# Moving the four adds of one pooling group from GpSimd to VectorE in a hybrid decoder step

## The chip, the cores and the metric

The kernel runs on one core of a Trainium2 chip. The metric is the device time of one execution in microseconds (us), taken as the median of several runs; lower is better. The core has five engines with queues of their own: TensorE (PE in the profile, its weight loads PEld), VectorE (DVE), ScalarE (ACT), GpSimd (POOL) and SyncE (SP), which here only issues DMAs.

## The reference

One inference step of a decoder trunk with one layer: a half-step SwiGLU FFN, a mixer, a second half-step FFN and a final RMSNorm, for one sequence of 512 new tokens and for 8 samples with one token each (520 tokens in all, 1024 features, float32). The mixer has two parallel parts, a Mamba-2 state-space part (SSD) and the pooling part that the change touches:

```python
POOL_WINDOWS = (2, 4, 8, 16)
...
    u = jnp.concatenate([prefix.astype(u_new.dtype), u_new], axis=1)
    cs = jnp.cumsum(u.astype(jnp.float32), axis=1)
    cs = jnp.concatenate([jnp.zeros((b, 1, POOL_DIM), jnp.float32), cs], axis=1)
    end = cs[:, POOL_STATE + 1:]
...
    for gi, w in enumerate(POOL_WINDOWS):
        sl = slice(gi * POOL_GROUP_DIM, (gi + 1) * POOL_GROUP_DIM)
        start = POOL_STATE + 1 - w
        win_sum = end[..., sl] - cs[:, start:start + T, sl]
        cnt = jnp.minimum(w, pos + 1).astype(jnp.float32)
        outs.append(win_sum / cnt[None, :, None])
    pooled = jnp.concatenate(outs, axis=-1) - u_new.astype(jnp.float32)
```

Each of four groups of 128 channels takes the mean over its last 2, 4, 8 or 16 tokens, minus the token itself. The result goes through a 128x128 matrix for each group, and then with the SSD part through the output projection `w_out`.

## The kernel before

Features lie on the 128 partitions and tokens along the free dimension, in two halves of 260 tokens (`HALVES`). Every float32 product of a weight and an activation is made of three matmuls on split operands (`mm3`, lines 123 to 128): a weight tile `raw` is rounded to `whi` by ScalarE (L113), and the rest `wlo = raw - whi` is made by VectorE (L114). The kernel runs FFN 1, the mixer and FFN 2 one after the other; TensorE is the engine that hardly pauses.

The mixer is a list of steps written out by hand. The strings `CONV_PLAN`, `GATE_PLAN` and `LAST_PLAN` name them in order, and `run` calls them:

- `p0` to `p3`: `pooling(g)`, a projection `inproj` of one group (48 matmuls into two PSUM banks), its copy to the tile `PU` by VectorE (`evac`, L703 to L705), and the window sums. For a window of 16, four adds with steps 1, 2, 4 and 8 make tiles `PW3_1`, `PW3_2`, `PW3_4` and `PW3_8`, each 128 partitions by about 650 elements. Then GpSimd mends the first tokens (L827, L828) and copies the new state out (L829, L830).
- `c0` to `c3`: `centre`, mean minus token (VectorE L834, L838, ScalarE L837). `m0` to `m3`: `mix`, the 128x128 product (L844 to L847).
- `A0` to `A7`: `ssd_a` for one chunk of 128 tokens and one of two head groups: two banks `pb` and `px` are filled by TensorE, a tile `ab` of 128x1024 is loaded by DMA (L954) and turned into decays by VectorE (L971), ScalarE (L969, L973, L974) and a last product on VectorE (L980); VectorE makes `xdt` from `px` (L976) and GpSimd makes `we` (L958) and `xw` (L979).
- `B0` to `B7`: `ssd_b`: TensorE makes `yo`, `pst` and `yd` from these; GpSimd scales the state `hst` (L1001), VectorE adds to it (L1002), puts `yo` and `yd` together in `E` (L1005, L1006) and adds into `X` (L1009).
- `z0` to `z7`: gate projections (tiles `inz`), 48 matmuls each, evacuated by VectorE (L1019). `o`, `g` and `h`: the output projection `w_out` in three blocks of four steps (`wout`, tiles `wo`), each half of a feature block added to `h` by VectorE (L1029). The block `g` (`wo1`) is followed by `h` (`wo2`) in `LAST_PLAN`.

The change sits in `p3`. The steps around it, as the plans give them:

```python
    "c3 X1 m2 A3 B2 e0"
...
    "A4 z0 B3 z1 m3 z2 B4 z3 s2 A5 ...
```

Two things decide the order on the engines. First, the whole program is recorded and then put in order at build time by a scheduler with a timeline model of its own (`schedule_with_timeline_sim=True`); each engine then runs its list strictly in order. An edit of one instruction's engine can so reorder other instructions. Second, all PSUM tiles of the mixer come from one pool of eight banks (`ppm`, through `bank`). The first matmul into a tile waits until the last reader of the bank's former tile is done. Which former tile that is comes from the same build-time model.

Of the kernel before, what the change touches and what calls it, by code (L numbers as in the profile page):

```python
# [12 lines left out]
ALU = mybir.AluOpType  # L13
# [37 lines left out]
LP = SAMPLE_P + 16 * NS  # L51
# [610 lines left out]
def mixer(tc, ins, outs, e):  # L662
    nc = tc.nc
# [29 lines left out]
    def inproj(src, name):  # L693
        wh, wl = load_unit(src, D, f"in{name}")
        bs = [bank(f"in{name}{b}") for b in range(2)]
        for b, hs in enumerate(HALVES):
            for k in range(KD):
                mm3(bs[b][:, :HB], ws(wh, k), ws(wl, k), xh[:, k, hs], xl[:, k, hs], k == 0, k == KD - 1)
        return bs

    def evac(bs, buf, off, soff, sstep):
        nb = SEQ - HB
        nc.vector.tensor_tensor(out=buf[:, off : off + HB], in0=bs[0][:, :HB], in1=r[:, :HB], op=ALU.mult)  # L703
        nc.vector.tensor_tensor(out=buf[:, off + HB : off + SEQ], in0=bs[1][:, :nb], in1=r[:, HB:SEQ], op=ALU.mult)
        nc.vector.tensor_tensor(out=buf[:, soff : soff + sstep * (NS - 1) + 1 : sstep], in0=bs[1][:, nb:HB],  # L705
                                in1=r[:, SEQ:NT], op=ALU.mult)
# [104 lines left out]
    def pooling(g):  # L811
        w = WINDOWS[g]
        bs = inproj(ins["w_in"][12 + g], f"p{g}")
        U = cv[0].tile([P, LP], F32, tag="cu", bufs=6, name=f"PU{g}")
        us = U[:, SAMPLE_P:LP].rearrange("p (b j) -> p b j", j=16)
        nc.gpsimd.memset(U[:, 0:PAST], 0.0)
        nc.gpsimd.tensor_copy(us[:, :, 0:PAST], spool[:, g])
        evac(bs, U, PAST, SAMPLE_P + PAST, 16)
        cur, step = U, 1
        while step < w:  # L820
            nxt = cv[0].tile([P, LP], F32, tag="cu", bufs=6, name=f"PW{g}_{step}")
            lo = 2 * step - 1
            nc.gpsimd.tensor_tensor(out=nxt[:, lo:LP], in0=cur[:, lo:LP], in1=cur[:, lo - step : LP - step], op=ALU.add)
            cur, step = nxt, 2 * step
        first = slice(PAST, PAST + w - 1)
        sx = slice(SAMPLE_P + PAST, LP, 16)
        nc.gpsimd.tensor_tensor(out=cur[:, first], in0=cur[:, first], in1=rcnt[:, : w - 1], op=ALU.mult)  # L827
        nc.gpsimd.tensor_tensor(out=cur[:, first], in0=cur[:, first], in1=U[:, first], op=ALU.subtract)  # L828
        nc.gpsimd.tensor_copy(npp[:, g], U[:, SEQ : SEQ + PAST])  # L829
        nc.gpsimd.tensor_copy(spool[:, g], us[:, :, 1:16])  # L830

        def centre():
            for q in (slice(PAST + w - 1, PAST + SEQ), sx):
                nc.vector.scalar_tensor_tensor(out=cur[:, q], in0=cur[:, q], scalar=1.0 / w, in1=U[:, q],  # L834
                                               op0=ALU.mult, op1=ALU.subtract)
            for q, t in ((slice(PAST, PAST + SEQ), slice(0, SEQ)), (sx, slice(SEQ, NT))):
                nc.scalar.copy(catp[:, 0, g, t], cur[:, q])  # L837
                nc.vector.tensor_tensor(out=catp[:, 1, g, t], in0=cur[:, q], in1=catp[:, 0, g, t].bitcast(F32),  # L838
                                        op=ALU.subtract)

        def mix():
            for b, hs in enumerate(HALVES):
                ps = bank(f"pm{g}{b}")
                mm3(ps[:, :HB], ws(wph, g), ws(wpo, g), catp[:, 0, g, hs], catp[:, 1, g, hs], True, True)  # L844
                sc = v("pool_scale", g)
                nc.scalar.activation(out=catp[:, 0, g, hs], in_=ps[:, :HB], func=AF.Copy, scale=sc)
                nc.vector.scalar_tensor_tensor(out=catp[:, 1, g, hs], in0=ps[:, :HB], scalar=sc,  # L847
                                               in1=catp[:, 0, g, hs].bitcast(F32), op0=ALU.mult, op1=ALU.subtract)
        return centre, mix
# [225 lines left out]
    def outs_a():  # L1075
# [10 lines left out]
        "y": lambda j: sample_bc(),  # L1086
        "X": sample_x,
        "p": lambda j: pooled.append(pooling(j)),
        "c": lambda j: pooled[j][0](),
        "m": lambda j: pooled[j][1](),  # L1090
# [112 lines left out]
```

## Time and profile before

| | before |
|---|---|
| median of 3 runs | 988.39 us (987.58 to 988.75) |
| profiled execution, time | 988.96 us |
| its span in the profile | 987.1 us |
| TensorE matmul, busy | 971.9 us (98%) |
| VectorE, busy | 797.2 us (81%) |
| ScalarE, busy | 555.2 us (56%) |
| GpSimd, busy | 91.2 us (9%) |

The span is the stretch from the first to the last instruction of the profiled execution; 1.86 us of its 988.96 us lie outside of it. A timeline row gives the start of an instruction, or of several alike that follow each other (xN), the time that it took, engine, line, operation, output<-input, and in brackets how long the engine had been idle and what ended that. Instructions of one engine overlap by some 0.07 us at their ends, so the distance from one start to the next is a little less than the duration.

### The profile page before, as it was taken

To read this page: it belongs to the slowest core of one execution; us is meant where nothing else is said; L and a number is where in the kernel's file an instruction comes from. 1 tells how busy PE (TensorE), PEld (TensorE's weight loads), DVE (VectorE), ACT (ScalarE), POOL (GpSimd) and SP (SyncE) were. 2 spreads that over 40 slices of the span, in tenths; PEclk is the share of its full clock that TensorE was granted. 3 is DMA by queue.
4 is the path that set the end of the run, shared out by engine and by line. 5 is a ranking of instruction groups with operands and counts; after the bars stand their busy time and mean duration, and the time that the engine had idled before them with its cause. 6 is when DMAs were issued, how large, how long until landed. Compare 5 with 4: busy or idle time off the path is not lost.

```text
span 987.1 us, 19460 instructions
## 1 busy us (share of the span) xinstructions
PE 971.9 (98%) x7868; PEld 952.7 (97%) x7868; DVE 797.2 (81%) x1287; ACT 555.2 (56%) x1019; POOL 91.2 (9%) x161
## 2 busy tenths in 40 slices
PE   9999999999999999999999999999999999999996
PEld 8999999999999999999899999999999999999995
DVE  6999656996569688789978997999967899668876
ACT  7766414664236465685668574666643566534653
POOL 0000000000000000156522000100012000120000
PEclk9999999999999999999999999999999999999998
DMA  7523232323222232262335232523346423453212
GB/s 217 178 86 124 90 100 72 129 86 129 86 86 97 75 126 99 86 192 100 122 114 187 77 131 86 154 101 128 121 118 195 146 99 116 123 179 124 92 64 88
DMA packets 43963, 116.57 MB, mean 118 GB/s; under 512 B 6552, under 2 KB 14680, under 8 KB 43872
## 3 DMA queue, kind: packets, MB, share of 16 engines
q1 hardware_dynamic: 39824, 104.18, 31.3%
q0 software_dynamic: 3776, 11.01, 4.3%
q8 instruction: 62, 1.02, 0.4%
q14 instruction: 29, 0.24, 0.1%
q10 hardware_dynamic: 272, 0.13, 0.0%
HBM read 107.96 MB, written 7.34 MB: 117 GB/s over the span
## 4 chain that ended last, share of the span: by engine, by line
PE 89%; DVE 4%; ACT 3%; DMA 1%; issue 1%; POOL 0%; SPq 0%; DVEq 0%; ACTq 0%
PE A L128 8%; PE A L124 8%; PE A L127 8%; PE dn L128 7%; PE dn L124 7%; PE dn L127 7%; PE BE L128 6%; PE BE L127 6%; PE BE L124 6%; PE wo L124 2%; PE wo L128 2%; PE wo L127 2%; PE P L257 2%; PE inz L124 2%; PE inz L128 2%; PE inz L127 2%
## 5 line engine op out<-in xcount | busy, mean ns | idle before, releaser
L124 PE MATMUL dn<-g,whi_1d 128*128 128x260 f32 x352 | 99.5, 283 | 0.2 <-DVE td L421 0.2
L127 PE MATMUL dn<-g,whi_1d 128*128 128x260 f32 x352 | 99.7, 283 | 0.0
L128 PE MATMUL dn<-g,wlo_1d 128*128 128x260 f32 x352 | 99.4, 282 | 0.0
L421 DVE SCALAR_TENSOR_TENSOR td<-dn,r_f 128x520 f32<-128x520 f32 x40 | 27.9, 699 | 72.8 <-PE dn L128 72.8
L128 PE MATMUL dn<-g,wlo_2d 128*128 128x260 f32 x256 | 72.7, 284 | 1.0 <-DVE wlo_2d L114 1.0
L127 PE MATMUL dn<-g,whi_2d 128*128 128x260 f32 x256 | 72.4, 283 | 0.0
L124 PE MATMUL dn<-g,whi_2d 128*128 128x260 f32 x256 | 72.4, 283 | 0.0
L124 PEld LDWEIGHTS dn<-g,whi_1d 128*128 128x128 f32 x352 | 66.2, 188 | 0.4 <-DVE td L421 0.4
L128 PEld LDWEIGHTS dn<-g,wlo_1d 128*128 128x128 f32 x352 | 66.4, 189 | 0.0
L127 PEld LDWEIGHTS dn<-g,whi_1d 128*128 128x128 f32 x352 | 66.3, 188 | 0.0
L351 ACT COPY ac<-A 128x260 f32<-128x260 f32 x123 | 45.5, 372 | 28.7 <-PE A L128 27.2
L113 ACT CAST whi_1d<-raw_1d 128x1024 fp32r<-128x1024 f32 (+1 forms) x24 | 23.4, 980 | 67.1 <-PE dn L127 54.3
L312 DVE TENSOR_TENSOR s<-raw 128x1024 f32<-128x1024 f32 x39 | 47.6, 1221 | 5.8 <-DMA raw<-in_w2gu 5.8
L128 PEld LDWEIGHTS dn<-g,wlo_2d 128*128 128x128 f32 x256 | 48.2, 188 | 1.2 <-DVE wlo_2d L114 1.2
L124 PEld LDWEIGHTS dn<-g,whi_2d 128*128 128x128 f32 x256 | 48.4, 189 | 0.0
L127 PEld LDWEIGHTS dn<-g,whi_2d 128*128 128x128 f32 x256 | 48.3, 189 | 0.0
L257 PE MATMUL P<-xg_f,raw 128*128 128x260 f32 x192 | 44.2, 384 | 0.8 <-ACT tg L270 0.6
L257 PEld LDWEIGHTS P<-xg_f,raw 128*128 128x128 f32 x192 | 35.8, 190 | 6.7 <-ACT tg L270 1.0
L124 PE MATMUL wo<-catg,whi_wo 128*128 128x260 f32 x128 | 37.2, 291 | 0.0
L124 PE MATMUL inz<-xh_mx,whi_inz 128*128 128x260 f32 x128 | 36.8, 288 | 0.1
L124 PE MATMUL inx<-xh_mx,whi_inx 128*128 128x260 f32 x128 | 36.5, 285 | 0.0
L128 PE MATMUL wo<-catg,wlo_wo 128*128 128x260 f32 x128 | 36.2, 283 | 0.0
(1351 smaller groups left out, 3954.8 us busy)
## 6 DMA issues: line engine op xcount, KB each, us to landing
raw<-in_w2gu SPq DMA_DIRECT2D x44, 512.0 KB, 4.5
raw<-in_w1gu SPq DMA_DIRECT2D x41, 512.0 KB, 4.4
raw_1d<-in_w1d SPq DMA_DIRECT2D x16, 512.0 KB, 4.4
raw_2d<-in_w2d SPq DMA_DIRECT2D x16, 512.0 KB, 4.4
raw_wo<-in_w_out SPq DMA_DIRECT2D x12, 512.0 KB, 4.6
ab<-scr_acs SPq DMA_DIRECT2D x8, 512.0 KB, 4.3
h<-in_state_ssm SPq DMA_DIRECT2D x16, 256.0 KB, 3.4
raw_inz<-in_w_in SPq DMA_DIRECT2D x8, 512.0 KB, 4.0
```

The lines of the kernel that those rows point to most:

```text
L113: cast = nc.scalar.copy(h, src)
L124: first = nc.tensor.matmul(ps, whi, xhi, start=start, stop=False, **kw)
L127: nc.tensor.matmul(ps, whi, xlo, start=False, stop=False, **kw)
L128: nc.tensor.matmul(ps, wlo, xhi, start=False, stop=stop, **kw)
L257: mm = nc.tensor.matmul(self.banks[f, u][b][:, :HB], ws(self.raw[f][:, u], j + 4 * q), xg[:, slot[q]], start=j == q == 0, stop=j == 3 and ...
L312: nc.vector.tensor_tensor(out=s1, in0=diag, in1=up0, op=ALU.add)
L351: nc.scalar.copy(keep, out[:, :HB])
L421: nc.vector.scalar_tensor_tensor(out=t, in0=banks[d][:, :, :HB], scalar=-0.5, in1=self.nx[3].rearrange("p (b t) -> p b t", b=2), op0=ALU.mult,
```

## The change

In `pooling`, the adds of group 3 (window 16) are issued to VectorE; those of groups 0 to 2 stay on GpSimd. Nothing else is edited. From line 824 on, the changed kernel's line numbers are higher by one.

```diff
         while step < w:
             nxt = cv[0].tile([P, LP], F32, tag="cu", bufs=6, name=f"PW{g}_{step}")
             lo = 2 * step - 1
-            nc.gpsimd.tensor_tensor(out=nxt[:, lo:LP], in0=cur[:, lo:LP], in1=cur[:, lo - step : LP - step], op=ALU.add)
+            eng = nc.vector if g == 3 else nc.gpsimd
+            eng.tensor_tensor(out=nxt[:, lo:LP], in0=cur[:, lo:LP], in1=cur[:, lo - step : LP - step], op=ALU.add)
             cur, step = nxt, 2 * step
```

## Prediction
> **What bounds the kernel now.** I read the page first: the busy times, then the chain that ended last.
>
> ```profile
> PE 971.9 (98%) x7868; PEld 952.7 (97%) x7868; DVE 797.2 (81%) x1287; ACT 555.2 (56%) x1019; POOL 91.2 (9%) x161
> ...
> PE 89%; DVE 4%; ACT 3%; DMA 1%; issue 1%; POOL 0%; SPq 0%; DVEq 0%; ACTq 0%
> ```
>
> TensorE is busy nearly all the time and makes 89% of the chain. VectorE's 81% and GpSimd's 9% matter only where TensorE waits for them. So I asked for TensorE's waits between 440 and 600 us, the mixer, and then for its timeline where they are.
>
> ```profile
> 476.98 1.09 PE L995 MATMUL yd<-ab,xdt 128*64 128x128 f32 x16 [0.43 <-DVE U L703]
> ...
> 478.65 0.30 PE L944 MATMUL pb<-ident,BC 128*128 128x128 f32 x1 [0.58 <-DVE U L705]
> ...
> 479.83 0.55 PE L952 MATMUL px<-ident,X 128*128 128x128 f32 x3 [0.66 <-DVE xdt L976]
> 480.43 0.39 PE L124 MATMUL inz<-xh_mx,whi_inz 128*128 128x260 f32 x1
> ```
>
> In brackets stand the only three: 0.43, 0.58 and 0.66 us, 1.67 us in all, each ended by VectorE. All are bank waits. The `yd` of step B2 and the `pb` of A4 take the banks whose last readers are the copies L703 and L705 of the projection `inx`; the `px` of A4 takes the bank that `xdt` L976 reads. The `inz` at 480.43 (z0) starts without a gap, but in the built program its bank is the one that `yo` of B2 held, read by L1005. So VectorE's queue is late here and TensorE is held by it. Its timeline at that place, with the clean durations of the same operations from later on:
>
> ```profile
> 465.00 0.17 DVE L705 TENSOR_TENSOR PU<-inp,r_mx 128x8 f32<-128x8 f32 x1
> ...
> 465.67 2.00 DVE L114 TENSOR_TENSOR wlo_inz<-raw_inz,whi_inz 128x1024 fp32r<-128x1024 f32 x1
> ...
> 468.50 1.40 DVE L980 TENSOR_TENSOR ab<-ab,scm 128x1024 f32<-128x1024 f32 x1
> ...
> 470.84 0.69 DVE L1002 TENSOR_TENSOR hst<-pst,hst 128x512 f32<-128x512 f32 x1 [0.34 <-POOL hst L1001]
> 471.45 2.61 DVE L1009 SCALAR_TENSOR_TENSOR X<-X,h,E 128x128 f32<-128x128 f32 x4
> 474.76 1.83 DVE L971 TENSOR_SCALAR ab<-ab,tok 128x128 f32<-128x128 f32 x2 [0.70 <-ACT E L964]
> 476.51 0.42 DVE L703 TENSOR_TENSOR U<-inx,r_mx 128x260 f32<-128x260 f32 x1
> 476.85 1.25 DVE L971 TENSOR_SCALAR ab<-ab,tok 128x128 f32<-128x128 f32 x6
> ...
> 479.70 0.68 DVE L1005 TENSOR_TENSOR E<-yo,E 128x512 f32<-128x512 f32 x1
> 480.30 1.26 DVE L114 TENSOR_TENSOR wlo_inz<-raw_inz,whi_inz 128x1024 fp32r<-128x1024 f32 x1
> ...
> 484.36 1.12 DVE L1009 SCALAR_TENSOR_TENSOR X<-X,h,E 128x128 f32<-128x128 f32 x4
> 485.42 1.21 DVE L980 TENSOR_TENSOR ab<-ab,scm 128x1024 f32<-128x1024 f32 x1
> ...
> 500.30 0.86 DVE L971 TENSOR_SCALAR ab<-ab,tok 128x128 f32<-128x128 f32 x4
> ```
>
> L1005 (479.70) ends at 480.38, and `inz` starts 0.05 us later. L703 ends at 476.93, and `yd` starts 0.05 us later. So 0.05 us lies between a reader's end and the matmul.
>
> Many of these rows are too long. A 128x1024 product takes 1.21 (485.42), but 2.00 at 465.67. Four L1009 take 1.12 (484.36), but 2.61 at 471.45. Four L971 take 0.86 (500.30), but two take 1.83 at 474.76. GpSimd's timeline says why:
>
> ```profile
> 465.31 1.27 POOL L823 TENSOR_TENSOR PW<-PU 128x654 f32<-128x654 f32 x1
> 466.53 1.28 POOL L830 COPY spool<-PU 128x120 f32<-128x120 f32 x1
> 467.78 1.04 POOL L979 TENSOR_TENSOR xw<-xdt,we 128x512 f32<-128x512 f32 x1
> 468.78 2.03 POOL L1001 TENSOR_TENSOR hst<-hst,cd 128x512 f32<-128x512 f32 x1
> 470.77 2.62 POOL L823 TENSOR_TENSOR PW<-PW 128x652 f32<-128x652 f32 x2
> 474.61 0.20 POOL L958 TENSOR_TENSOR we<-ab,tok 128x8 f32<-128x8 f32 x1 [1.23 <-DMA ab<-scr_acs]
> 474.77 1.54 POOL L823 TENSOR_TENSOR PW<-PW 128x640 f32<-128x640 f32 x1
> ...
> 479.44 1.04 POOL L1001 TENSOR_TENSOR hst<-hst,cd 128x512 f32<-128x512 f32 x1
> 480.44 2.02 POOL L979 TENSOR_TENSOR xw<-xdt,we 128x512 f32<-128x512 f32 x1
> ```
>
> The adds of the group stand at 465.31, 470.77 (two) and 474.77. The long VectorE rows start while an add runs and come free when it ends, and the reverse: `hst` (468.78, 2.03 against 1.04 at 479.44) waits for VectorE's product to end. [...] Rows with an operand in PSUM (L1005, 0.68) are not stretched.
>
> **The change, part by part.** *The order.* In the built programs TensorE has the same list in both. On VectorE the four adds go into the stretch between the last copy of `PU` (ends 465.17) and L703 (476.51). Besides, the scheduler reorders what follows: the split L114 of `inz` (480.30) now stands ahead of `xdt`, and so ahead of L1005; the four L971 of `ab` for A3 stand between `xdt` and L1005. ScalarE makes the decays of A4 first and those of A3 later. On SP one small output DMA goes ahead of one weight load. I take the end of L1005 as the clock of this place, because z0 cannot start before it, and count what VectorE has to do up to there.
>
> *Added: four adds.*
>
> ```profile
> L834 DVE SCALAR_TENSOR_TENSOR PW<-PW,PU 128x505 f32<-128x505 f32 x1 | 0.7, 689 | 0.4 <-POOL PW L823 0.4
> ...
> L312 DVE TENSOR_TENSOR s<-raw 128x1024 f32<-128x1024 f32 x39 | 47.6, 1221 | 5.8 <-DMA raw<-in_w2gu 5.8
> ```
>
> From 689 ns for 505 elements and 1221 for 1024 follow 1.03 ns an element, so 0.84 us for 654, and 0.76 from start to start: +3.0 us.
>
> *Moved ahead of L1005: the split L114.* 480.30 to 481.48, where the next instruction starts in the trace: +1.2 us.
>
> *Removed: the stretching by the adds.* L114 at 465.67, 2.00 - 1.26 = 0.74; the four L1009, 2.61 - 1.12 = 1.49; two L971, 1.75 from start to start against 0.4 = 1.35. Together -3.6 us.
>
> *Removed: two idle times of VectorE*, 0.34 for GpSimd's `hst` and 0.70 for ScalarE's `E`. GpSimd reaches `hst` earlier without the adds, and L971 no longer follows `E` at once: -1.0 us. Also the 0.19 us by which `xw` (467.78) stretched L980 at 468.50.
>
> *Added: new collisions.* GpSimd still has two `hst` and two `xw` of 1.04 us each, now against a VectorE with more SBUF work. The first pair starts about 466.1, when its small copies are over, and meets L114 and the second add. The second `hst` comes behind a copy that waits for L705 and so starts together with L834 and L114. The second `xw` waits for `xdt` alone and starts the moment it ends, where the four L971 stand. None of this is in the trace of before; the bounds are nothing and all four whole, 4.2 us. The rows say that who comes first holds the other for what is left, so more than half: I take 0.9 for the first pair, 0.6 and 0.9 for the others, 2.4 us.
>
> The sum: 480.38 + 3.0 + 1.2 - 3.6 - 1.0 - 0.2 + 2.4 = 482.2, and z0 starts at about 482.2 instead of 480.43: **+1.8 us**, in which the three waits are contained. TensorE does not win the 1.67 us: the first two waits shrink or go, and one before `inz` takes their place. With the bounds: 479.8 and 484.0, so -0.6 to +3.5 us.
>
> *Does ScalarE hold VectorE there?*
>
> ```profile
> 474.09 1.28 ACT L964 ACTIVATE E<-ab 64x512 f32<-64x512 f32 x2 [3.04 <-DVE X L1009]
> ...
> 476.68 1.26 ACT L969 ACTIVATE ab<-ab,tok 128x128 f32<-128x128 f32 x4
> 477.85 1.03 ACT L113 CAST whi_inz<-raw_inz 128x1024 fp32r<-128x1024 f32 x1
> ```
>
> The `ab` of A4 has landed when GpSimd's `we` starts at 474.61. In the new order ScalarE then makes `we`, four L969 (1.26) and the `whi` cast (1.03): about 477.2, when VectorE, at my count, reaches the split. It is just in time and costs nothing; if the load of `ab` lands late (on SP it stands behind a weight load that waits for the L114 of 465.67), each us of it counts here, since `xdt` stands behind.
>
> *A second place.* The banks are dealt out anew. I compared, in the two built programs, what each TensorE instruction waits for. Outside the stretch above, up to some 492 us, one wait differs: the first matmul of `wo2`. In the kernel before its bank was last read by the residual add L1029 for `wo1_5`, half 1; in the changed kernel by that for `wo1_7`, half 1, whose matmuls come right ahead of it.
>
> ```profile
> 592.80 0.43 DVE L1029 TENSOR_TENSOR h<-wo,h 128x260 f32<-128x260 f32 x1
> ...
> 597.01 0.43 DVE L1029 TENSOR_TENSOR h<-wo,h 128x260 f32<-128x260 f32 x1 [0.29 <-PE wo L128]
> ```
>
> ```profile
> 596.69 0.28 PE L128 MATMUL wo<-catg,wlo_wo 128*128 128x260 f32 x1
> 596.81 0.28 PE L124 MATMUL wo<-catg,whi_wo 128*128 128x260 f32 x1
> ```
>
> The first add of the fence is the old release, 3.6 us before the matmul at 596.81; the second is the new one, which ends at 597.44. The matmul would start at 597.49: **+0.7 us**. It can be no less than 0.5, since the add cannot start before its matmul ends (596.69 + 0.28 = 596.97) and takes 0.43. It can be more if VectorE comes late: it was idle for only 0.29 us before this add. I take 0.65.
>
> *Nothing else.* On GpSimd 91 us are busy in the span, and nothing queued there but `hst` and `xw` is needed soon. On SP an output DMA moves ahead of a weight load:
>
> ```profile
> 468.12 0.38 SPq L1079 DMA_DIRECT2D out_nps<-spool  x1
> ```
>
> It takes 0.38 us to issue, and the load behind it is needed only at z4.
>
> Together 1.8 + 0.65 = +2.4 us. The profiled time of 988.96 would become 991.4; against the median of the runs, 988.39, I forecast **990.8 us**. A difference of 0.2% (2.0 us) is about the least that a measurement of this kernel can tell from no change.
>
> **Rivals.** *The engines hardly collide.* If GpSimd's four operations fall beside VectorE's PSUM rows, which are not stretched, z0 starts at 479.8: -0.6 + 0.65, so 988.4, not slower. For it: some of VectorE's operations in this stretch read PSUM. Against it: `xw` is released by the very instruction ahead of the L971. It decides at collisions below some 2 us. [...]
>
> *The faster adder wins.* If VectorE gets ahead of TensorE at all its banks, the three waits go and the bank of `wo2` is free in time: -1.67 us, 986.7. For it: on GpSimd an add takes 1.27 us, on VectorE 0.84. [...] Against it: VectorE is the late engine at this place, and the wait of `wo2` stands in the program.
>
> *VectorE stays behind.* The delay of 1.8 us goes on into B3, whose `yd` needs the L980 of A3.
>
> ```profile
> 486.55 0.75 DVE L838 TENSOR_TENSOR catp<-PW,catp 128x512 fp32r<-128x512 f32 x2
> ...
> 488.13 1.09 PE L995 MATMUL yd<-ab,xdt 128*64 128x128 f32 x16
> ```
>
> In the trace of before it takes 6.25 us from the end of L1005 (480.38) to the end of that L980 (485.42 + 1.21). In the new order the split (1.2) and the four L1009 (1.1) no longer lie between, but the two L838 (0.7) do: 4.65 us, so it ends at about 486.9. `yd` of B3 would start at 488.13 + 1.8 = 489.9: 3 us to spare. Should collisions or late ScalarE rows take 5 us there, the excess of 2 us adds: 992.8.
>
> **How the numbers follow.** The forecast's case 0.62, of it 0.54 above +2.0 us and 0.08 below; hardly any collision 0.24 (no change); faster adder 0.06, a good half of it beyond 0.2% with the scatter of the runs; VectorE behind 0.08 (slower). That makes slower 0.62, same 0.34, faster 0.04. The range: its lower end is the case without collisions, 988.4, less 0.4 for the scatter of the runs (987.58 to 988.75): 988.0; its upper end is the bound of the collisions, 3.5 + 0.65, less a little: 992.3. Left out are the faster adder (0.06), about 0.06 of the case without collisions and most of VectorE behind. The forecast's case alone goes from 989.5 to 992.3.
>
> **What would show it.** In the profile of the changed kernel: four VectorE adds of 0.8 to 1.1 us; no L114, L1009 or L971 stretched at the places quoted, but L971 ahead of L1005 stretched by `xw`; a TensorE gap of some 2 us or more before the first `inz`, ended by L1005; a gap of some 0.65 us before the first `wo2`, ended by L1029. The forecast is wrong if the gaps before `yd`, `pb`, `px` and `inz` sum to 1.7 us or less, or if `wo2` starts without one.

## The result, and the profile after

The changed kernel takes 992.18 us (median of 6 runs, 991.01 to 992.54), the kernel before 988.38 us (median of 6 runs). The ratio is 1.0036, 95% interval 1.0026 to 1.0047: slower by 3.8 us. The forecast was 990.8 us with a range of 988.0 to 992.3. The direction and the two places were right, but of the three parts of the loss the largest was not in the forecast. The profiled execution took 992.34 us, with a span of 990.6 us against 987.1.

The page of the changed kernel, busy times and the chain that ended last:

```profile
PE 974.4 (98%) x7868; PEld 955.1 (96%) x7868; DVE 797.8 (81%) x1291; ACT 555.0 (56%) x1019; POOL 85.7 (9%) x157
...
PE 90%; DVE 6%; ACT 2%; DMA 1%; issue 1%; POOL 0%; DVEq 0%; SPq 0%; ACTq 0%
```

TensorE's busy time rises by 2.5 us although it does the same matmuls, and VectorE's share of the chain goes from 4% to 6%. GpSimd has 5.5 us less. TensorE's waits between 440 and 620 us (what waits, for whom, total, times, longest):

```profile
PE inz L124 <- DVE E L1006: 1.8, 1, 1.8
PE px L953 <- DVE xdt L977: 1.0, 1, 1.0
PE wo L124 <- DVE h L1030: 0.6, 1, 0.6
```

Of the three bank waits of before only the one at `px` is left, and it is longer; the one at z0's first `inz` is new, and so is the one at `wo`. TensorE's timeline at the first place, as far as B3, and below it the `yo` of B3 in the kernel before:

```profile
476.52 1.09 PE L996 MATMUL yd<-ab,xdt 128*64 128x128 f32 x16
...
479.07 0.55 PE L953 MATMUL px<-ident,X 128*128 128x128 f32 x3 [0.97 <-DVE xdt L977]
481.42 0.58 PE L124 MATMUL inz<-xh_mx,whi_inz 128*128 128x260 f32 x1 [1.81 <-DVE E L1006]
481.80 0.42 PE L127 MATMUL inz<-xl_mx,whi_inz 128*128 128x260 f32 x1
482.02 0.42 PE L128 MATMUL inz<-xh_mx,wlo_inz 128*128 128x260 f32 x1
...
484.62 0.30 PE L128 MATMUL inz<-xh_mx,wlo_inz 128*128 128x260 f32 x1
484.75 0.28 PE L124 MATMUL inz<-xh_mx,whi_inz 128*128 128x260 f32 x1
...
488.70 1.05 PE L990 MATMUL yo<-BC,hst 128*128 128x128 f32 x8
```

```profile
486.29 0.94 PE L989 MATMUL yo<-BC,hst 128*128 128x128 f32 x7
```

The waits before `yd` and `pb` are gone, `px` waits 0.97 us, and z0's first `inz` waits 1.81 us and starts at 481.42 instead of 480.43: 0.99 us late. Then something happens that no row of before shows. The `inz` matmuls stand 0.22 us apart (481.80, 482.02) up to 484.62 and 0.12 us apart from then on, and the `yo` of B3 comes at 488.70 instead of 486.29, 2.41 us late. So 1.42 us are lost after z0 has started, with no wait. Two stretches of time, first of the kernel before, then of the changed kernel; the columns after the stretch are its length, busy time and instructions of PE, PEld, DVE, ACT and POOL, then the granted TensorE clock, DMA share and GB/s:

```profile
477.80:481.20 3.40, 2.11 (x18) 1.47 (x15) 3.40 (x9) 3.40 (x8) 2.71 (x5) 1.00 0.21 57
481.40:484.60 3.20, 3.20 (x29) 3.20 (x28) 3.20 (x8) 2.25 (x7) 1.51 (x2) 1.00 0.43 150
```

```profile
477.80:481.20 3.40, 0.84 (x6) 0.41 (x4) 3.40 (x7) 3.40 (x10) 2.69 (x3) 1.00 0.21 66
481.40:484.60 3.20, 3.18 (x14) 3.18 (x15) 3.20 (x7) 2.48 (x8) 0.20 (x1) 0.50 0.38 127
```

In the changed kernel the granted clock is 0.50 while these matmuls run; in the kernel before it is 1.00. In the 3.4 us ahead of it TensorE was busy for 0.84 us only, in the kernel before for 2.11.

VectorE's timeline of the changed kernel at this place, then GpSimd's:

```profile
465.35 0.84 DVE L824 TENSOR_TENSOR PW<-PU 128x654 f32<-128x654 f32 x1
...
466.70 1.72 DVE L114 TENSOR_TENSOR wlo_inz<-raw_inz,whi_inz 128x1024 fp32r<-128x1024 f32 x1
...
468.94 1.07 DVE L824 TENSOR_TENSOR PW<-PW 128x652 f32<-128x652 f32 x1
...
471.33 0.82 DVE L824 TENSOR_TENSOR PW<-PW 128x648 f32<-128x648 f32 x1
...
473.21 1.13 DVE L1010 SCALAR_TENSOR_TENSOR X<-X,h,E 128x128 f32<-128x128 f32 x4
474.26 0.81 DVE L824 TENSOR_TENSOR PW<-PW 128x640 f32<-128x640 f32 x1
...
477.20 1.21 DVE L114 TENSOR_TENSOR wlo_inz<-raw_inz,whi_inz 128x1024 fp32r<-128x1024 f32 x1
478.33 0.68 DVE L977 TENSOR_TENSOR xdt<-px,tok 128x512 f32<-128x512 f32 x1
478.94 1.83 DVE L972 TENSOR_SCALAR ab<-ab,tok 128x128 f32<-128x128 f32 x4
480.69 0.68 DVE L1006 TENSOR_TENSOR E<-yo,E 128x512 f32<-128x512 f32 x1
```

```profile
477.21 2.10 POOL L1002 TENSOR_TENSOR hst<-hst,cd 128x512 f32<-128x512 f32 x1
...
479.42 1.08 POOL L980 TENSOR_TENSOR xw<-xdt,we 128x512 f32<-128x512 f32 x1
```

The adds take 0.81 to 1.07 us, and the four `X` rows (L1010) 1.13 instead of 2.61. The split at 477.20 and the four L972 stand ahead of E<-yo (L1006), which ends at 481.37; `inz` starts 0.05 us later. GpSimd's `xw` (479.42, 1.08 us) runs beside these four L972, which take 1.83 instead of the 0.86 of the four at 475.33.

The second place on TensorE:

```profile
599.99 0.36 PE L124 MATMUL wo<-catg,whi_wo 128*128 128x260 f32 x1 [0.61 <-DVE h L1030]
```

The first `wo2` matmul waits for the residual add of the block before it, as the built program said. It starts at 599.99 instead of 596.81, 3.18 us late; 2.41 of these come from above, 0.77 are made here.

So the profile gives 0.99 + 1.42 + 0.77 = 3.18 us of the 3.5 us by which the spans differ. The remaining 0.3 us lie elsewhere and were not followed.

### The profile page after: what moved, and what is told of

It is laid out like the page before. It is cut to its first block, busy times and chain, and to the rows that moved or that the text cites. A ratio compares the mean times of both kernels' runs of the same rounds, so it can differ in the third digit from the quotient of the medians.

```text
span 990.6 us, 19461 instructions
## 1 busy us (share of the span) xinstructions
PE 974.4 (98%) x7868; PEld 955.1 (96%) x7868; DVE 797.8 (81%) x1291; ACT 555.0 (56%) x1019; POOL 85.7 (9%) x157
## 4 chain that ended last, share of the span: by engine, by line
PE 90%; DVE 6%; ACT 2%; DMA 1%; issue 1%; POOL 0%; DVEq 0%; SPq 0%; ACTq 0%
PE A L128 8%; PE A L124 8%; PE A L127 8%; PE dn L128 7%; PE dn L124 7%; PE dn L127 7%; PE BE L128 6%; PE BE L127 6%; PE BE L124 6%; PE P L257 4%; PE wo L124 2%; PE wo L128 2%; PE wo L127 2%; PE inz L124 2%; PE inz L127 2%; PE inz L128 2%
## 5 line engine op out<-in xcount | busy, mean ns | idle before, releaser
L127 PE MATMUL inz<-xl_mx,whi_inz 128*128 128x260 f32 x128 | 36.8, 288 | 0.0
L128 PE MATMUL inz<-xh_mx,wlo_inz 128*128 128x260 f32 x128 | 36.7, 287 | 0.0
```

What stands on the lines that cost most here:

```text
L127: nc.tensor.matmul(ps, whi, xlo, start=False, stop=False, **kw)
L128: nc.tensor.matmul(ps, wlo, xhi, start=False, stop=stop, **kw)
```

## Experiments

All times are medians. The kernel before was run beside each group (988.4 to 988.8 us); the ratio is to it.

| run | adds of group 3 on | what else is changed | us | ratio, 95% interval |
|---|---|---|---|---|
| changed kernel | VectorE | nothing | 992.18 | 1.0036 (1.0026 to 1.0047) |
| fill | VectorE | 7 spare matmuls | 993.05 | 1.0043 (1.0030 to 1.0055) |
| fill3 | VectorE | 10 spare matmuls in the gap | 990.81 | 1.0023 (1.0014 to 1.0031) |
| behind | VectorE | split of z2 later | 990.05 | 1.0016 (1.0007 to 1.0025) |
| ahead | GpSimd | split of z2 earlier | 991.98 | 1.0030 (1.0020 to 1.0041) |
| late_g | GpSimd | adds later | 990.14 | 1.0017 (1.0008 to 1.0026) |
| late_v2 | VectorE | adds later | 992.51 | 1.0044 (1.0030 to 1.0057) |
| tuned | VectorE | three things later | 988.21 | 0.9996 (0.9987 to 1.0004) |
| tuned_b | GpSimd | the same three later | 990.07 | 1.0013 (1.0003 to 1.0022) |
| best3 | VectorE | one step further | 988.08 | 0.9992 (0.9984 to 1.0001) |
| best3b | GpSimd | one step further | 989.03 | 1.0004 (0.9995 to 1.0013) |
| best4 | VectorE | two steps further | 986.68 | 0.9980 (0.9971 to 0.9989) |

**Does the idle time halve the clock?** The first try (fill) put seven matmuls into `ssd_a`, behind the `px` transposes of A4:

```diff
+        if (c, g) == (0, 1):
+            for _ in range(7):
+                nc.tensor.matmul(pb[:, 2 * P : 3 * P], BC[:, g, cs], BC[:, 2 + g, cs], start=True, stop=True)
```

> The changed kernel with seven matmuls whose result nobody reads, queued on TensorE behind the px transposes of step A4, where TensorE waits for VectorE before z0. In the build they also shift the banks, so that the first matmul of wo2 takes a bank that was read long before. Theory (TensorE's clock is halved because it idles there): E<-yo of B2 still ends at about 481.4, z0 still starts at 481.4, but the granted clock stays 1.0 and the inz matmuls stand 0.12 us apart from nearly the first; -1.4 us there, and -0.8 us at wo2, so some 990.0 us against 992.2 of the changed kernel, although TensorE has more to do. Rival (the halved clock has another cause, such as the work of the other engines or chance): clock 0.5 again for 3.4 us behind z0, only the 0.8 us at wo2 come back, 991.4. Rival (the wo2 gap isn't a matter of banks): a gap of 0.6 us before wo2 stays.

It missed its aim: the scheduler set the seven matmuls at 489.4 to 491.0, behind z0, not into the gap. The gap before z0 stayed at 1.81 us and the clock at 0.50 behind it. The time rose by 0.9 us: the matmuls add 1.6 us, and the 0.77 us at `wo2` go. So it still answers the question on `wo2`: here, in the built program, the bank was last read by the add of `wo1_4`, and there is no wait at `wo2`. That wait is a matter of banks.

The second try (fill3) traces ten of them ahead of the first reader of `pb` and holds `px` and z0 behind them:

```diff
+        if (c, g) == (0, 1):
+            for _ in range(10):
+                held["fill"] = nc.tensor.matmul(pb[:, 2 * P : 3 * P], ...)
...
-        for q in range(4):
+        with tc.issue_after(held["fill"].ins) if (c, g) == (0, 1) else nullcontext():
+            for q in range(4):
...
-        bs = inproj(ins["w_in"][16 + j], f"z{j}")
+        with tc.issue_after(held["fill"].ins) if j == 0 else nullcontext():
+            bs = inproj(ins["w_in"][16 + j], f"z{j}")
```

> The changed kernel with ten matmuls whose result nobody reads, held on TensorE between the pb matmuls and the px transposes of step A4, where TensorE waits for VectorE. The order on the other engines, z0's bank and wo2's bank are those of the changed kernel. Theory (the clock is halved because TensorE idles some 2.8 of the 3.4 us ahead of z0): E<-yo of B2 still ends at about 481.4 and z0 still starts then, but only some 0.6 to 1.2 us of idle time are left, the granted clock stays 1.0, the inz matmuls stand 0.12 us apart from nearly the first: 1.4 us less, 990.7 us, though TensorE does 2.2 us more. Rival (the halved clock has another cause): granted clock 0.5 behind z0 as before, 992.2 us. Rival (the ten matmuls push px and z0 back): z0 later than 481.6, 993 us or more.

TensorE's timeline and the two stretches of time:

```profile
477.92 2.40 PE L949 MATMUL pb<-BC 128*128 128x128 f32 x20
480.16 0.49 PE L957 MATMUL px<-ident,X 128*128 128x128 f32 x3
481.36 0.39 PE L124 MATMUL inz<-xh_mx,whi_inz 128*128 128x260 f32 x1 [0.71 <-DVE E L1010]
```

```profile
477.80:481.20 3.40, 2.85 (x26) 2.61 (x24) 3.40 (x7) 3.40 (x10) 2.63 (x3) 1.00 0.26 62
481.40:484.60 3.20, 3.20 (x27) 3.20 (x28) 3.20 (x7) 2.15 (x7) 0.20 (x1) 1.00 0.43 145
```

z0 starts at 481.36, as in the changed kernel, VectorE's order is the same, and the `wo2` wait is still there. But TensorE is busy for 2.85 us of the 3.4 ahead of z0, and the granted clock stays 1.00. The time is 990.81 us, where 990.7 was expected: TensorE does 2.2 us more and the kernel is faster than the changed one. What is left over before, 2.0 us, is near the 0.94 us at z0 (481.36 - 480.43) and the 0.77 us at `wo2`. The other executions agree: the mean granted clock over the span is 0.996 to 0.998 in all 11 of them, and 0.994 to 0.996 in the six of the changed kernel; 3.4 us at 0.50 make 0.002 of it. The halved clock is thus shown to come from TensorE's idle time at this place.

**Is it the adds or the order?** In "behind" the split of z2 may only be issued behind E<-yo of B2; the adds stay on VectorE:

```diff
+        with tc.issue_after(held["yoE"].ins) if j == 2 else nullcontext():
             bs = inproj(ins["w_in"][16 + j], f"z{j}")
```

> The changed kernel with one order imposed: the split wlo of z2 (1.1 us on VectorE) may be issued only behind E<-yo of B2, as in the kernel before; the four adds stay on VectorE and the wo2 bank stays the late one. Theory (the reordered split is what makes z0 late, the adds themselves are paid for by the stretching that goes): z0 starts at 480.3 instead of 481.4, TensorE idles some 1.2 us less, the clock stays 1.0, and the time is 992.2 - 1.1 - 1.4 = 989.7 us; the wo2 gap of 0.6 us stays. Rival (the adds themselves make VectorE late, and the split only fills a wait for GpSimd or ScalarE): z0 not before 481.2, halved clock, 992 us.

```profile
480.16 0.39 PE L124 MATMUL inz<-xh_mx,whi_inz 128*128 128x260 f32 x1 [1.89 <-DVE E L1006]
...
480.99 0.42 PE L124 MATMUL inz<-xh_mx,whi_inz 128*128 128x260 f32 x1
481.20 0.42 PE L127 MATMUL inz<-xl_mx,whi_inz 128*128 128x260 f32 x1
```

z0 starts at 480.16, earlier even than in the kernel before: the split was the reason for its lateness. But TensorE, which no longer waits before `px`, still idles for 1.89 us in one piece, and the clock falls all the same, a little later (0.21 us from row to row at 480.99). The expected 1.4 us did not come back in this profile. The time was 990.05 us where 989.7 was expected, 2.1 less than the changed kernel's, though only 1.3 are seen at z0; a wait of 1.0 us before `dn` in the second FFN stands in the profiles of the changed kernel and of the kernel before and not in this one, so parts of this size come and go for reasons that were not followed. The 11 executions lie in two groups, six from 989.4 to 990.1 us, the profiled one among them, and five from 991.0 to 991.8. What parts them is not shown, since only one has a trace.

In "ahead" the kernel before keeps its adds on GpSimd, and only `xdt` of A3 is put behind the split of z2:

```diff
...
+        if j == 2:
+            tc.add_manual_dep(held["xdt", 3, 0].ins, ends[1].name, ...)
```

> The kernel before, adds on GpSimd, with one order imposed: xdt of A3 may be issued on VectorE only behind the split of z2, as in the changed kernel. In the build E<-yo of B2 then comes first, the split second, xdt third; the px of A4 waits for E, and z0's bank is released by xdt; the banks of wo2 are as in the kernel before. Theory (a reader of z0's bank that comes 1.1 us later is enough, wherever the adds are made): z0 starts at about 481.5 instead of 480.4, TensorE idles 2.8 us between 476 and 481.5, its clock is halved for 3.4 us in most executions: 988.8 + 1.1 + 1.4 = 991.3 us, or 989.9 in those where the clock holds. Rival (the adds on VectorE are needed for the loss): within 0.5 us of the kernel before.

TensorE, then VectorE:

```profile
482.25 0.39 PE L124 MATMUL inz<-xh_mx,whi_inz 128*128 128x260 f32 x1 [1.83 <-DVE xdt L977]
...
482.60 0.41 PE L128 MATMUL inz<-xh_mx,wlo_inz 128*128 128x260 f32 x1
```

```profile
479.74 1.86 DVE L114 TENSOR_TENSOR wlo_inz<-raw_inz,whi_inz 128x1024 fp32r<-128x1024 f32 x1
481.52 0.68 DVE L977 TENSOR_TENSOR xdt<-px,tok 128x512 f32<-128x512 f32 x1
```

The reader of z0's bank (now `xdt`) ends at 482.20, z0 waits 1.83 us, and a row behind it takes 0.41 us, as under the halved clock of the changed kernel (0.42), not 0.28. 991.98 us: without any add moved, an order like the changed kernel's (here `xdt` comes last, there E<-yo) costs 3.3 us alone, nearly what the change costs. That was more than the 991.3 us expected; the split took 1.86 us, where it took 1.26 at 480.30 in the kernel before. Two of the eight executions took 990.4 and 990.6 us, not far from the 989.9 expected where the clock holds.

**Is the place of the adds the point?** Two versions move the step `c3` behind `A3 B2` and issue the adds there, once on GpSimd (late_g), once on VectorE and only behind E<-yo of B2 (late_v2):

```diff
-    "c3 X1 m2 A3 B2 e0"
+    "X1 m2 A3 B2 c3 e0"
...
         def centre():
+            if g == 3:
+                with tc.issue_after(held["yoE"].ins):   # late_v2 alone
+                    sums()                              # the adds and the mending of the first tokens
```

> The kernel before (adds on GpSimd) with the step c3 moved behind A3 and B2 in the list, and the adds of group 3 traced there, so that three of them come behind xw of A3 and hst of B2 on GpSimd. Theory (what bounds this place is VectorE's queue ahead of E<-yo of B2, whoever adds): VectorE loses there the 3.6 us of stretching and the two centre instructions of 0.7 us, the three waits of TensorE before yd, pb and px shrink below 0.3 us in sum, z0 starts at about 478.9, and the time is 988.4 - 1.5 = 986.9 us. Rival (GpSimd is in the way wherever the adds stand: xw or hst of B3 come late behind an add): a new wait of 1 us or more before pst or yo of B3, 988 us or more.

> The changed kernel (adds of group 3 on VectorE) with the step c3 moved behind A3 and B2, and all four adds issued only behind E<-yo of B2. Theory (the place of the adds is what counts, not the engine): z0 at about 478.9 as with the late adds on GpSimd, clock 1.0, no gap before wo2 since its bank is an early one here; 986.9 us, within 0.5 us of the late adds on GpSimd. Rival (VectorE has no room for 3 us anywhere near): the adds hold up L114, ab of A3 or catp, with waits of 1 us or more before inz, yd of B3 or pm, 988.5 us or more.

Both theories failed: 986.9 us was expected of each, 990.14 and 992.51 us came. Waits of late_g, its VectorE rows and a GpSimd row:

```profile
PE yd L1005 <- DVE ab L990: 1.7, 1, 1.7
PE px L962 <- ACT X L793: 0.8, 1, 0.8
```

```profile
481.19 3.44 DVE L1019 SCALAR_TENSOR_TENSOR X<-X,h,E 128x128 f32<-128x128 f32 x4
...
485.47 2.03 DVE L990 TENSOR_TENSOR ab<-ab,scm 128x1024 f32<-128x1024 f32 x1
```

```profile
479.92 2.74 POOL L830 TENSOR_TENSOR PW<-PW 128x652 f32<-128x652 f32 x2
```

z0 starts as early as TensorE can, but four L1019, beside the adds, now take 3.44 us instead of 1.12, the product L990 behind them, beside GpSimd's `hst` (485.39, 1.04 us), takes 2.03 instead of 1.21, and `yd` of B3 waits 1.7 us for it. The gain at z0 is given back at the next step. In late_v2 too `yd` of B3 waits, 2.2 us for the same product, then `px`, 1.2 us (its profiled execution was 3.5 us above its median, so only the places are read). My theory that only the queue ahead of z0 matters fell: VectorE is full from 465 to 495 us (busy for 28.9 of these 30 us in the kernel before), and what is put off must be something that nobody needs before that.

**An order that spares the adds.** "tuned" leaves the adds at their old place on VectorE and puts three things that are needed late behind E<-yo of B2: the centre of group 3, L971 for A4 and the split of z2. "tuned_b" does the same with the adds on GpSimd (of the diff the added conditions alone):

```diff
-    "c3 X1 m2 A3 B2 e0"
+    "X1 m2 A3 B2 c3 e0"
...
+            with tc.issue_after(held["yoE"].ins) if g == 3 else nullcontext():        # around centre
...
+        with tc.issue_after(held["yoE"].ins) if (c, g) == (0, 1) else nullcontext():  # around L971
...
+        with tc.issue_after(held["yoE"].ins) if j == 2 else nullcontext():            # around inproj of z2
```

> The changed kernel (four adds on VectorE, at their old place) with three things put behind E<-yo of B2 on VectorE: the centre of group 3 (0.7 us), L971's four operations for ab of A4 (0.8 us) and the split of z2 (1.1 us). Theory (what is in VectorE's queue ahead of E<-yo of B2 decides, and these three were not needed there): z0 starts at 481.4 - 2.6 = 478.8, within 0.6 us of where TensorE alone would start it; clock 1.0; the wo2 bank is one read earlier than in the changed kernel, gap 0 to 0.1; 986.9 us, faster than both kernels. Rival (VectorE is full over a longer stretch, and what is put off comes due at B3): z0 at 478.8, but a wait of 1 us or more for VectorE before yd of B3, 988.5 us.

> The kernel before (adds on GpSimd) with the same three things put behind E<-yo of B2. Theory: the adds cost VectorE about as much by stretching (3.6 us) as by being made there (3.0 us and collisions), so with the order the same in both, z0 starts within 0.6 us of the version with the adds on VectorE, and the times differ by less than 1 us. Rival (GpSimd is the better place): 1 us or more faster than with the adds on VectorE. Rival (VectorE is the better place): 1 us or more slower, with the stretching seen on L1009 and L971 again.

TensorE and VectorE of tuned:

```profile
479.55 0.39 PE L124 MATMUL inz<-xh_mx,whi_inz 128*128 128x260 f32 x1 [1.19 <-DVE E L1011]
```

```profile
476.68 2.21 DVE L977 TENSOR_SCALAR ab<-ab,tok 128x128 f32<-128x128 f32 x4 [0.39 <-ACT E L969]
```

z0 at 479.55: 1.9 us earlier than in the changed kernel, 0.9 earlier than in the kernel before, not the 2.6 expected, since L977 (ab of A3) fell on `xw` and `hst` of GpSimd and took 2.21 us instead of 0.86. 988.21 us, where 986.9 was expected, 4.0 us below the changed kernel with the adds on the same engine. Against the kernel before the interval holds 1. Two waits of tuned_b, two VectorE rows and two GpSimd rows:

```profile
PE yd L1000 <- DVE ab L985: 1.5, 1, 1.5
PE inz L124 <- DVE catp L851: 1.2, 1, 1.2
```

```profile
478.66 2.07 DVE L838 SCALAR_TENSOR_TENSOR PW<-PW,PU 128x497 f32<-128x497 f32 x2
...
487.38 2.01 DVE L985 TENSOR_TENSOR ab<-ab,scm 128x1024 f32<-128x1024 f32 x1
```

```profile
479.22 1.48 POOL L1006 TENSOR_TENSOR hst<-hst,cd 128x512 f32<-128x512 f32 x1
...
487.27 1.04 POOL L1006 TENSOR_TENSOR hst<-hst,cd 128x512 f32<-128x512 f32 x1 [4.46 <-DVE X L1016]
```

With the adds on GpSimd and the same three conditions the time is 990.07 us, where less than 1 us from tuned was expected. So VectorE is the better place for the adds here, by 1.9 us, but z0 is not the reason: it starts at 478.79 in tuned_b, without a wait and earlier than in tuned. TensorE loses behind it, 1.2 us before a later `inz` and 1.5 us before `yd` of B3. The two VectorE rows are stretched (the two centre operations take 0.74 us in tuned, a 128x1024 product 1.21), the first beside GpSimd's `xw` (478.22, 1.05 us) and `hst`, the second beside the next `hst`, neither beside an add. The rest of the order was left to the scheduler and differs between the two kernels, so how much of the 1.9 us is the engine and how much the order is not shown.

Two more steps follow the wait that is left each time. "best3" puts L971 for A3 behind E<-yo of B2 too, and the three late things behind the last product of A3 ("best3b" with the adds on GpSimd); "best4" puts L971 and the last product for A4 and the split of z3 behind E<-yd of B3, because best3 waited there (its one wait in the mixer, 1.0 us of the `inz` of z2 for E<-yd L1019):

```diff
 best3
+                for i in held["l971"]:                       # L971 of A3, behind E<-yo of B2
+                    tc.add_manual_dep(i.ins, yoE.ins.name, ...)
-        with tc.issue_after(held["yoE"].ins) ...             # the three late things
+        with tc.issue_after(held["G", 3, 0].ins) ...          # G: the product L980 of A3
 best4
+                for i in (*held["l971"], held["G", 0, 1]):    # those of A4, behind E<-yd of B3
+                    tc.add_manual_dep(i.ins, ydE.ins.name, ...)
+        with tc.issue_after(held["ydE"].ins) ...              # around inproj of z3
```

> The version with the adds on VectorE and the order mended, taken one step further: the four L971 of ab for A3 go behind E<-yo of B2 as well, and the centre of group 3, L971 for A4 and the split of z2 behind the product that ends ab of A3. Theory (order in VectorE's queue decides): E<-yo of B2 ends at 476.9 instead of 479.5, z0 starts where TensorE alone would have it, at about 478.2, the clock stays 1.0, ab of A3 is ready at 485 and yd of B3 needs it at 486: 988.2 - 1.3 = 986.9 us. Rival (VectorE is full): what is gained at z0 comes back as a wait of 1 us before yd or px of the next steps, 988 us or more.

> The same order with the adds on GpSimd as in the kernel before. Theory (the adds on GpSimd stretch VectorE by 3 to 4 us between 465 and 485 us, and in the good order that is what is left to gain): E<-yo of B2 ends about 1 us later than with the adds on VectorE, waits before yd of B2 or B3 of 0.4 to 1.5 us, 1 to 2 us slower than with the adds on VectorE, 988 to 989 us. Rival (with the order mended the engine doesn't matter): within 0.5 us.

> The last order with the adds on VectorE, and on top of it L971 and the last product of ab for A4 and the split of z3 behind E<-yd of B3, since the wait of 1.0 us that was left stands before z2, whose bank that instruction reads. Theory: E<-yd of B3 ends at about 492.2, z2 could start at 494.0 and no longer waits; 988.1 - 1.0 = 987.1 us, faster than the kernel before by 1.6 us. Rival (VectorE is full in the whole stretch): the wait turns up again before yd of B4 or a later bank, 988 us.

best3 misses its 986.9 us by what its rival says, a wait of 1.0 us before z2; best3b is 0.95 us slower, with intervals that overlap. The waits expected for best3b before `yd` of B2 or B3 did not come. It waits 0.7 us before `px` and 0.8 us before z2, and in its profiled execution `inz` rows behind them take 0.42 us (from 496.40), as under the clock of 0.50 in the changed kernel. best4 meets its forecast of 987.1: 986.68 us, faster than the kernel before, ratio 0.9980 (0.9971 to 0.9989). Its order with the adds on GpSimd was not run. Its two stretches of time:

```profile
477.80:481.20 3.40, 3.40 (x31) 3.40 (x30) 3.32 (x9) 3.38 (x10) 0.94 (x1) 1.00 0.50 171
481.40:484.60 3.20, 3.20 (x30) 3.20 (x29) 3.20 (x9) 2.70 (x8) 0.20 (x1) 1.00 0.00 0
```

TensorE is busy without a break in both, at full clock.

## Why the prediction was right or wrong

- **What bounds the kernel**: right. TensorE is held by VectorE at PSUM banks; of the four matmuls named, the `px` of A4 and the first `inz` of z0 wait in the changed kernel.
- **The four adds, +3.0 us**: they took 0.84, 1.07, 0.82 and 0.81 us; less the overlap of some 0.07 us each 3.26 us, of which 0.23 is a collision (1.07 against 0.84). Right.
- **The split moved ahead, +1.2 us**: 477.20 to 478.33, 1.13 us. Right, and "behind" and "ahead" show that it decides where z0 starts.
- **The stretching removed, -3.6 us, and the idle times, -1.2 us**: right; L1010 is clean, and VectorE no longer waits for `hst` or `E`. ScalarE held nothing up, as forecast: its `whi` cast ended at 476.48, ahead of the split at 477.20.
- **Collisions, +2.4 us**: mis-sized. On VectorE they cost 0.46 (L114 at 466.70), 0.23 (the second add) and 0.97 (L972), 1.66 us. The second `hst` was to cost 0.6 and cost nothing: it started at 477.21, 0.01 us behind the split, and it was `hst` that waited (2.10 us), not the split (1.21). With 1.66 the sum of the prediction gives 481.4, and E<-yo ended at 481.37. So z0 came 0.99 us late, not 1.8.
- **The second place, +0.65 us**: 0.77 us, of which 0.61 as a gap. Right.
- **The step that failed** is the one that took a late start of z0 as its whole price ("z0 starts at about 482.2 instead of 480.43: +1.8 us, in which the three waits are contained"). The three small waits became one of 1.81 us behind one of 0.97, and TensorE's clock was halved for 3.4 us: +1.42 us more. The trace of before did not show it: there the granted clock is 1.00 at this place, with three waits that add up to 1.67 us, not 2.78. In the changed kernel's trace the clock is at 0.50 for 3.41 us, from 481.22 to 484.64, and the waits of 0.97 and 1.81 us lie between 478.10 and 481.42.
- **Rivals.** "The engines hardly collide" and "the faster adder wins" did not come; neither did "VectorE stays behind": `yd` of B3 has no wait in the changed kernel. The sum of the forecast's case, 2.4 us, came out too small by the clock (+1.42) and too large by the collisions (-0.75). That the time still fell inside the range is luck: the upper end, 992.3, stood for collisions at their bound, and what brought the time to 992.18 was the clock, for which the range had no room.

## What to carry to other kernels

When a change gathers TensorE's waits into a few microseconds, ask of the stretch behind them whether the clock holds: the price of a late start can be more than the start (here 1.42 us behind a start that was 0.99 us late). Where a scheduler orders the program, moving an operation to another engine is two changes, the operation's cost and a new order with new banks; here an imposed order alone cost 3.3 us, and under conditions that were the same for both the kernels with the adds on VectorE were faster by 1.9 and by 0.95 us (the latter with intervals that overlap). These parts do not simply add up to the 3.8 us of the change. Before an add is given to the engine that is late, see what stands ahead of the late instruction and isn't needed there, and follow the wait that is left from step to step, as long as its engine still has something to put off.

## What was not expected of the hardware

- The granted clock of TensorE went to 0.50 for 3.4 us where TensorE had been busy for 0.84 of the 3.4 us before (changed kernel), and stayed 1.00 where it had been busy for 2.11 (before) and 2.85 (fill3). How much idle time it takes isn't settled: in best3b two waits of 0.7 and 0.8 us, which ended 1.1 us apart (494.72 and 495.80), were followed by `inz` rows of 0.42 us, as under the halved clock, and in late_g one of 1.7 us (until 487.56) by a clock of 1.00 from 487.5 to 491.

```profile
PE inz L124 <- DVE E L1018: 0.8, 1, 0.8
PE px L956 <- ACT X L793: 0.7, 1, 0.7
```

- In the changed kernel's trace the granted clock is recorded at 1.00 for 474.453 us, at 0.50 for 3.413 us and at 1.00 for another 498.346 us; in the trace of the kernel before at 1.00 for 976.212 us. The three long stretches are 139.01, 146.01 and 286.03 times the 3.413 us; why is not shown. In the 3.41 us ahead of the halving TensorE was busy, by its rows, for 0.83 us (changed kernel), 0.9 (ahead), 1.5 (behind) and about 2.0 (best3b); in the 3.41 us ahead of the late `yd` of late_g, for 1.68, and there the clock stayed at 1.00. So this busy time alone does not decide these cases. What parts the executions of "behind" and "ahead" into groups is not shown.

- The split, first by 0.01 us at 477.20, took its 1.21 us, and `hst`, at 477.21, took 2.10 instead of the 1.04 at 466.30: here the one that came first held the other for 1.06 us.
